# One decoder block on one core: in four groups of the feed-forward, VectorE instead of TensorE turns the other half of the hidden tiles

## The chip, the cores and the metric

The kernel runs on one NeuronCore of a Trainium2 chip, as one program and one launch. The metric is device time in microseconds (us), the median over runs of the same kernel. An engine is named by its role: TensorE (PE in the profile; its weight loads are PEld), VectorE (DVE), ScalarE (ACT), GpSimd (POOL), SyncE (SP), which issues nearly all DMAs.

## The reference

A decoder block on x of 512 tokens by 1,024 channels, float32: a token mixer of two branches (retention and forgetting attention), then the feed-forward that this change touches.

```python
        x = x + merged @ w_out[l]
        h2 = rmsnorm(x, g_ffn[l])
        ff = (jax.nn.silu(h2 @ w_gate[l]) * (h2 @ w_up[l])) @ w_down[l]
        x = x + ff
```

w_gate and w_up are 1,024 by 2,816, w_down is 2,816 by 1,024.

## The kernel before, in words

Every float32 operand of a large product is split into a high part (a cast to the matmul format, on ScalarE) and a low part (the rest, on VectorE), and a product is the sum of three matmuls: high by high, low by high, high by low.

**Gate and up.** The 2,816 hidden columns are taken in six groups, g = 0 to 4 of 512 columns and g = 5 of 256. A group's result is a 2 by 2 block product over halves of the tokens and halves of the weights, done in seven block products instead of eight. Their operands on the token side (A11, A12, A21, A22 and the sums S1 to S4) stand ready in `xfh` and `xfl`; those on the weight side are the blocks B11, B12, B21, B22, loaded for each group by SyncE, and sums of them that VectorE makes in place (`sum_of`, L947). Each weight block has two halves, v = 0 and 1. `part` makes high and low of one half (ScalarE's cast L938, VectorE's subtraction L939, called "low" below) in a ring of three buffers (`ring_parts`), so the cast of a half waits until the matmuls on the half three before it are through.

`gu` is one block product: four k-tiles j by two token tiles tp by three terms, 24 matmuls with a 128x128 stationary tile and 512 moving columns. The first 12 use half v = 0, the last 12 half v = 1. In a group the products follow one another as A12 (into the banks `y_`, tile name sc), A11 (`x_`), S1 (`z_`), S2 (`x_`), S3 (`x_`), S4 (`z_`), A22 (`x_`); `x_`, `z_` have the tile name acc. S2 and S3 go on adding in the banks that the product before left, so `keep` (ScalarE, L1048) first copies those banks to `us`. TensorE's order is pinned as the code is written (`mm`, `turn`); VectorE's mostly by `queue`; SyncE issues DMAs in code order, and a DMA that must wait holds all behind it; the rest of ScalarE's order is the scheduler's.

**Turning the hidden tiles.** `hs[g]` holds four tiles of 128 tokens by 512 hidden columns (they lie in `us`). The product with w_down needs them with hidden columns on partitions, in `pf`. In groups 1 to 4 (for the tiles of group g - 1 = 0 to 3) the columns are handled in two ways. The first two of the four 128-column tiles go through TensorE: `put_h` issues eight 128x128 transposes (L75, into bank tp) between the products A12 and A11, and two ScalarE copies (L1023) bring them to `pf`. The last two go through VectorE: `turn_squares` turns 32x32 squares (L1030) of a token tile, tokens 0 and 1 ahead of S1's sums, tokens 2 and 3 between the low parts of S2, into the tile `squares`, and `put_squares` has SyncE place them with 16 DMAs of 32 KB (L1037). The tiles of groups 4 and 5 go through TensorE alone.

After the groups, `prepare` and `p_sums` split the tiles of `pf` for the product with w_down.

Of the kernel before, what the change touches and what calls it, by code (L numbers as in the profile page):

```python
# [17 lines left out]
P = 128  # L18
# [35 lines left out]
def block_kernel(ctx: ExitStack, tc, x, xT, c_early, c_tab, c_late, w_qf, w_tok, w_vg, w_a, w_y, w_o, w_gu, w_gl, w_dn, w_dh, out):  # L54
# [880 lines left out]
    def part(raw, pinned_=True):  # L935
        w2 = raw.shape[-1]
        h, l = (f[:, :w2] for f in ring_parts())
        nc.scalar.copy(out=h, in_=raw)  # L938
# [14 lines left out]
    def gu(os, parts, slot, new, w, by_bank=False, middle=None):  # L953
        steps = [(j, tp) for j in range(4) for tp in range(2)]
        for i, (j, tp) in enumerate(sorted(steps, key=lambda s: s[1]) if by_bank else steps):
# [9 lines left out]
    parts_of = {}  # L965

    def prepare(k):
# [14 lines left out]
        ph, pl = hl[:, 0, :], hl[:, 1, :]  # L982
        prepare.last = nc.scalar.copy(out=ph, in_=pf[:, k, :])
        if n > 0:
            after(prepare.last, cast)
        prepare.low = tt(out=pl, in0=pf[:, k, :], in1=f32(ph), op=ALU.subtract)
        parts_of[k] = (h, l, ph, pl)

    def p_sums(j):

        fx = wq.tile([P, 4, HT], F32, name="fx", tag="b1")
        a11, a21, a12, a22 = (pf[:, 2 * j + m2, s2 * HT:s2 * HT + HT] for m2 in range(2) for s2 in range(2))
# [5 lines left out]
        split_x(j, slice(A12, A22 + 1), pf[:, 2 * j + 1, :].rearrange("p (s t) -> p s t", s=2))  # L998
# [19 lines left out]
    def put_h(g, cs):  # L1018
        for c in cs:
# [3 lines left out]
            nc.scalar.copy(out=pf[:, 4 * g + c, :], in_=pb)  # L1023
# [3 lines left out]
    def turn_squares(g, ts):  # L1027

        for t in ts:
            queue(nc.vector.transpose(out=squares[g].rearrange("p b c t j -> p c b t j")[:, :, :, t, :], in_=hs[g][t][:, 2 * P:4 * P].rearrange("p (c b j) -> p c b j", c=2, b=4)))  # L1030

    def put_squares(g):

        for a in range(4):
            for b in range(4):
                to = pf[32 * b:32 * b + 32, 4 * g + 2:4 * g + 4, :].rearrange("p c (t a j) -> p (c t) a j", t=NT, a=4)
                nc.sync.dma_start(out=to[:, :, a, :], in_=squares[g][32 * a:32 * a + 32, b].rearrange("p c t j -> p (c t) j"))  # L1037
# [4 lines left out]
    for g, w in enumerate(GROUPS):  # L1042
# [3 lines left out]
        def keep(slot, os):  # L1046
            for tp in range(2):
                nc.scalar.copy(out=us[tp][:, slot, :], in_=os[tp][:, :w])  # L1048

        if g == 0:  # L1050
# [7 lines left out]
            pf = fp.tile([P, NF, S], F32, name="pf")  # L1058
        else:
            gu(y_, ahead[g], A12, True, w)  # L1060
            put_h(g - 1, (0, 1))
            second = [ahead[g, 1], part(raws[g][B11][1])]
            if g - 1 in SQUARES:
                squares[g - 1] = xp.tile([P, 4, 2, NT, 32], F32, name="squares", tag="s4")
                turn_squares(g - 1, (0, 1))
# [30 lines left out]
        parts = sums_in_parts(g, B12, B22)  # L1096
        if g == 0:
# [4 lines left out]
        gu(x_, parts, S3, False, w)  # L1102
        keep(2, x_)
        parts = [part(raws[g][B22][v]) for v in range(2)]
        if g + 1 < len(GROUPS):
            load_group(g + 1, (B22,))
        gu(z_, parts, S4, False, w)
        parts = sums_in_parts(g, B11, B21)
        if g + 1 < len(GROUPS):
            load_group(g + 1, (B11,))  # L1110
        for tp in range(2):
# [3 lines left out]
        gu(x_, parts, A22, False, w, by_bank=True)  # L1115
# [267 lines left out]
```

## Time and profile before

| what | us |
|---|---|
| median of 3 runs | 702.68 (702.62 to 703.54) |
| profiled execution | 702.11 |
| its span, first to last instruction | 700.3 |
| TensorE busy in the span | 693.4 (99%) |
| VectorE, ScalarE, GpSimd busy | 526.7, 372.0, 72.7 |

The span is what the profiler's records cover; the other 1.8 us lie around it. A matmul's record is longer than its turn on the engine, since matmuls overlap: the pace is read from one start to the next. "Busy" of TensorE says therefore only that something was in flight.

### The profile page before, as it was taken

What the parts mean: (1) busy time and instruction counts of PE and PEld (TensorE: products, weight loads), DVE (VectorE), ACT (ScalarE), POOL (GpSimd) and SP (SyncE); (2) the same over time, 40 slices, a digit from 0 to 9 for tenths busy, and PEclk for the clock granted to TensorE, in tenths of its full rate; (3) what the DMA queues carried; (4) which work ended last, traced back from release to release, by engine and by line L of the source; (5) the groups of instructions that cost most, each with busy time, mean ns of one, the idle gap of its engine ahead of it and who ended that gap; (6) DMA issues with size and microseconds to landing.
All of it is one profiled execution on the core that took longest, in us unless ns stands there. A gap on an engine that the chain in (4) does not pass through costs nothing.

```text
span 700.3 us, 9534 instructions
## 1 busy us (share of the span) xinstructions
PE 693.4 (99%) x3567; PEld 579.6 (83%) x3567; DVE 526.7 (75%) x861; ACT 372.0 (53%) x562; POOL 72.7 (10%) x90
## 2 busy tenths in 40 slices
PE   9999999999999999999999999999999999999997
PEld 6878988888878777888887888888888898888997
DVE  6898487754788776648979897878888878457694
ACT  6767353232567666325566665565656576344341
POOL 0004940201122120000130000000000000000000
PEclk9999999999999999999999999999999999999999
DMA  8900412222433311238411506153341533321321
GB/s 278 420 28 31 122 61 91 83 82 93 135 108 90 105 62 61 90 117 299 185 61 34 208 11 217 43 150 121 73 168 23 157 121 105 119 77 61 100 81 62
DMA packets 41551, 79.40 MB, mean 113 GB/s; under 512 B 20248, under 2 KB 20888, under 8 KB 40992
## 3 DMA queue, kind: packets, MB, share of 16 engines
q1 hardware_dynamic: 41360, 78.77, 33.3%
q8 instruction: 28, 0.46, 0.3%
q14 instruction: 19, 0.16, 0.1%
q10 hardware_dynamic: 144, 0.02, 0.0%
HBM read 73.52 MB, written 2.11 MB: 108 GB/s over the span
## 4 chain that ended last, share of the span: by engine, by line
PE 94%; DVE 2%; ACT 1%; DMA 1%; issue 1%; POOL 0%; SPq 0%; POOLq 0%; DVEq 0%; ACTq 0%
PE acc L72 70%; PE sc L72 16%; PE tp L72 5%; PE tp L75 3%; DMA raw<-in_w_tok_dram 1%; POOL cb L680 0%; DMA cb<-cd 0%; DVE tq L667 0%; DVE pr L688 0%; DVE sg L737 0%; DVE wl L155 0%; ACT ps L938 0%; ACT tk L659 0%; DVE pr L692 0%; DVE blk L407 0%
## 5 line engine op out<-in xcount | busy, mean ns | idle before, releaser
L72 PE MATMUL acc<-ps,xfh 128*128 128x512 f32 (+1 forms) x576 | 169.1, 374 | 0.1
L72 PEld LDWEIGHTS acc<-ps,xfh 128*128 128x128 f32 x576 | 105.2, 188 | 21.8 <-ACT us L1048 2.4
L939 DVE TENSOR_TENSOR ps<-b,ps 128x1024 fp32r<-128x1024 f32 (+1 forms) x84 | 94.8, 1136 | 30.4 <-ACT ps L938 29.2
L938 ACT CAST ps<-b 128x1024 fp32r<-128x1024 f32 (+1 forms) x84 | 82.5, 982 | 51.6 <-PE acc L72 36.2
L72 PE MATMUL acc<-ps,xfl 128*128 128x512 f32 (+1 forms) x288 | 107.1, 372 | 0.0
L154 ACT CAST wh<-raw 128x1024 fp32r<-128x1024 f32 (+1 forms) x44 | 46.1, 1049 | 85.1 <-PE acc L72 80.7
L155 DVE TENSOR_TENSOR wl<-raw,wh 128x1024 fp32r<-128x1024 f32 (+1 forms) x44 | 57.8, 1315 | 17.6 <-ACT wh L154 17.5
L72 PEld LDWEIGHTS acc<-ps,xfl 128*128 128x128 f32 x288 | 54.3, 188 | 8.9
L72 PE MATMUL acc<-xh,wh 128*128 128x512 f32 x128 | 53.2, 416 | 0.0
L947 DVE TENSOR_TENSOR b<-b,b 128x1024 f32<-128x1024 f32 (+1 forms) x48 | 52.1, 1126 | 0.0
L72 PE MATMUL acc<-wh,xh 128*128 128x512 f32 (+2 forms) x144 | 50.4, 350 | 0.0
L72 PE MATMUL acc<-xh,wl 128*128 128x512 f32 x128 | 50.2, 392 | 0.0
L72 PE MATMUL acc<-xl,wh 128*128 128x512 f32 x128 | 50.0, 390 | 0.0
L72 PE MATMUL acc<-wh,xl 128*128 128x512 f32 (+2 forms) x144 | 49.4, 343 | 0.0
L72 PE MATMUL acc<-wl,xh 128*128 128x512 f32 (+2 forms) x144 | 49.3, 342 | 0.0
L72 PE MATMUL acc<-hl,ps 128*128 128x512 f32 x168 | 40.4, 389 | 0.0
L72 PEld LDWEIGHTS acc<-hl,ps 128*128 128x128 f32 x168 | 31.5, 188 | 6.6
L1048 ACT COPY us<-acc 128x512 f32<-128x512 f32 (+1 forms) x48 | 26.5, 552 | 18.6 <-PE acc L72 17.0
L977 DVE TENSOR_TENSOR ps<-raw,ps 128x1024 fp32r<-128x1024 f32 x14 | 17.1, 1223 | 21.6 <-ACT ps L974 21.6
L72 PEld LDWEIGHTS acc<-wh,xh 128*128 128x128 f32 x144 | 27.2, 189 | 3.5 <-ACT wh L154 0.2
L72 PEld LDWEIGHTS acc<-wh,xl 128*128 128x128 f32 x144 | 27.2, 189 | 3.2
L72 PEld LDWEIGHTS acc<-wl,xh 128*128 128x128 f32 x144 | 27.2, 189 | 2.9
(298 smaller groups left out, 1491.5 us busy)
## 6 DMA issues: line engine op xcount, KB each, us to landing
b<-in_w_gu_dram SPq DMA_DIRECT2D x40, 512.0 KB, 4.4
raw<-in_w_a_dram SPq DMA_DIRECT2D x16, 512.0 KB, 3.6
raw<-in_w_dn_dram SPq DMA_DIRECT2D x14, 512.0 KB, 4.3
blk<-in_w_vg_dram SPq DMA_DIRECT2D x8, 512.0 KB, 10.4
raw<-in_w_tok_dram SPq DMA_DIRECT2D x8, 512.0 KB, 3.6
raw<-in_w_y_dram SPq DMA_DIRECT2D x8, 512.0 KB, 3.5
raw<-in_w_o_dram SPq DMA_DIRECT2D x8, 512.0 KB, 3.7
raw<-in_w_dh_dram SPq DMA_DIRECT2D x4, 1024.0 KB, 4.8
```

The costliest lines, as they stand in the source:

```text
L72: in_order(nc.tensor.matmul(o, **kw))
L75: in_order(nc.tensor.transpose(out=o, in_=src, identity=ident))
L154: split_raw.last = (nc.scalar.copy(out=h[:, :width], in_=raw[:, :width]), tt(out=l[:, :width], in0=raw[:, :width], in1=f32(h)[:, :width], ...
L155: tt(out=l[:, :width], in0=raw[:, :width], in1=f32(h)[:, :width], op=ALU.subtract))
L938: nc.scalar.copy(out=h, in_=raw)
L939: low = tt(out=l, in0=raw, in1=f32(h), op=ALU.subtract)
L947: queue(tt(out=raws[g][b][v], in0=raws[g][b][v], in1=raws[g][c][v], op=ALU.add))
L977: tt(out=l, in0=raw, in1=f32(h), op=ALU.subtract)
L1048: nc.scalar.copy(out=us[tp][:, slot, :], in_=os[tp][:, :w])
```

## The change

- In groups 1 to 4, `put_h` is not called. `turn_squares` turns whole token tiles (512 columns instead of 256), and the tile `squares` holds half of the tokens at a time, in the same 4 KB of a partition (tag s4) twice a group. Token tiles 0 and 1 are turned where they were; token tiles 2 and 3 are turned in the third product's time, one ahead of each half of B22's parts.
- `put_squares` issues 16 DMAs of 32 KB for each half, 32 a group instead of 16: the first 16 behind the loads of B21, the second 16 in pieces of 5, 7 and 4 around the loads of B22 and B11 of the next group.
- The copies of A11's, S2's and S3's results (`keep` with slots 0, 1, 2) are placed by order behind the second cast of the parts made next (`part.cast`); in group 0 only that of S3.
- `gu` takes S2 and S3 with `by=2`: pairs of k-tiles, (j 0, 1 of tp 0), (j 0, 1 of tp 1), (j 2, 3 of tp 0), (j 2, 3 of tp 1), instead of alternating tp at each j. `by=4` is the earlier `by_bank`.
- `pf` is laid out with the token half ahead of the tile number.

```diff
-    def gu(os, parts, slot, new, w, by_bank=False, middle=None):
+    def gu(os, parts, slot, new, w, by=1, middle=None):
+
         steps = [(j, tp) for j in range(4) for tp in range(2)]
-        for i, (j, tp) in enumerate(sorted(steps, key=lambda s: s[1]) if by_bank else steps):
+        for i, (j, tp) in enumerate(sorted(steps, key=lambda s: (s[0] // by, s[1], s[0]))):
...
+    def turn_squares(g, t):
+
+        to = squares[g, t // 2].rearrange("p b c t j -> p c b t j")[:, :, :, t % 2, :]
+        queue(nc.vector.transpose(out=to, in_=hs[g][t].rearrange("p (c b j) -> p c b j", c=4, b=4)))
+
+    def place_of_squares(g, half):
+        squares[g, half] = xp.tile([P, 4, 4, 2, 32], F32, name="squares", tag="s4")
+
+    def put_squares(g, half, which=range(16)):
+
+        for i in which:
+            a, b = i // 4, i % 4
+            to = pf[32 * b:32 * b + 32, half, 4 * g:4 * g + 4, :].rearrange("p c (t a j) -> p (c t) a j", t=2, a=4)
+            nc.sync.dma_start(out=to[:, :, a, :], in_=squares[g, half][32 * a:32 * a + 32, b].rearrange("p c t j -> p (c t) j"))
...
-            put_h(g - 1, (0, 1))
+            if g - 1 not in SQUARES:
+                put_h(g - 1, (0, 1))
             second = [ahead[g, 1], part(raws[g][B11][1])]
             if g - 1 in SQUARES:
-                squares[g - 1] = xp.tile([P, 4, 2, NT, 32], F32, name="squares", tag="s4")
-                turn_squares(g - 1, (0, 1))
+                place_of_squares(g - 1, 0)
+                for t in range(2):
+                    turn_squares(g - 1, t)
                 gu(x_, second, A11, True, w)
...
         if g - 1 in SQUARES:
-            sums = [sum_of(g, B11, B22, v) for v in range(2)]
-            parts = [part(sums[0])]
-            turn_squares(g - 1, (2, 3))
-            parts.append(part(sums[1]))
-            put_squares(g - 1)
-        else:
-            parts = sums_in_parts(g, B11, B22)
-        gu(x_, parts, S2, False, w)
-        keep(1, x_)
+            put_squares(g - 1, 0)
+        parts = sums_in_parts(g, B11, B22)
+        gu(x_, parts, S2, False, w, by=2)
+        if g == 0:
+            keep(1, x_)
...
         parts = sums_in_parts(g, B12, B22)
+        if g:
+            keep(1, x_, part.cast)
...
-        gu(x_, parts, S3, False, w)
-        keep(2, x_)
-        parts = [part(raws[g][B22][v]) for v in range(2)]
+        gu(x_, parts, S3, False, w, by=2)
+        if g - 1 in SQUARES:
+            place_of_squares(g - 1, 1)
+        parts = []
+        for v in range(2):
+            if g - 1 in SQUARES:
+                turn_squares(g - 1, 2 + v)
+            parts.append(part(raws[g][B22][v]))
+        keep(2, x_, part.cast)
+        if g - 1 in SQUARES:
+            put_squares(g - 1, 1, range(5))
         if g + 1 < len(GROUPS):
             load_group(g + 1, (B22,))
+        if g - 1 in SQUARES:
+            put_squares(g - 1, 1, range(5, 12))
```

On TensorE, at the end of product A12 of group 1 (banks sc) and the start of A11 (banks acc); us_3534 and us_3535 are the two tiles of `us`, ctab holds the identity:

```order
 L72 MATMUL sc<-ps,xfl 128x512
 L72 MATMUL sc<-ps,xfh 128x512
-L75 MATMUL tp<-ctab,us_3534 128x128
-L75 MATMUL tp<-ctab,us_3535 128x128
...
 L72 MATMUL acc<-ps,xfh 128x512
 L72 MATMUL acc<-ps,xfl 128x512
```

The eight transposes are gone and A11 follows A12 directly; the same in groups 2 to 4.

On VectorE in group 2, from the turn of token tiles 0 and 1 to the low parts of S4, before. b_4066, b_3996 and b_4031 are the blocks B11, B12 and B22; L947 are sums in place (x2: both halves), L939 low parts:

```order
L1030 STREAM_TRANSPOSE squares<-us_3534 128x2x4x32
L1030 STREAM_TRANSPOSE squares<-us_3535 128x2x4x32
L947 TENSOR_TENSOR b_4066<-b_4066,b_3996 128x1024 x2
L939 TENSOR_TENSOR ps<-b_4066,ps 128x1024 x2
L947 TENSOR_TENSOR b_4066<-b_4066,b_4031 128x1024 x2
L939 TENSOR_TENSOR ps<-b_4066,ps 128x1024
L1030 STREAM_TRANSPOSE squares<-us_3534 128x2x4x32
L1030 STREAM_TRANSPOSE squares<-us_3535 128x2x4x32
L939 TENSOR_TENSOR ps<-b_4066,ps 128x1024
...
L939 TENSOR_TENSOR ps<-b_4031,ps 128x1024 x2
```

And of the changed kernel (B11, B12 and B22 are b_4067, b_3982 and b_4025 there):

```order
L1034 STREAM_TRANSPOSE squares<-us_3534 128x4x4x32
L1034 STREAM_TRANSPOSE squares<-us_3535 128x4x4x32
L947 TENSOR_TENSOR b_4067<-b_4067,b_3982 128x1024 x2
L939 TENSOR_TENSOR ps<-b_4067,ps 128x1024 x2
L947 TENSOR_TENSOR b_4067<-b_4067,b_4025 128x1024 x2
L939 TENSOR_TENSOR ps<-b_4067,ps 128x1024 x2
...
L1034 STREAM_TRANSPOSE squares<-us_3534 128x4x4x32
L939 TENSOR_TENSOR ps<-b_4025,ps 128x1024
L1034 STREAM_TRANSPOSE squares<-us_3535 128x4x4x32
L939 TENSOR_TENSOR ps<-b_4025,ps 128x1024
```

The first pair of turns is twice as wide in its old place; the second pair left S2's low parts and stands, twice as wide, one ahead of each low part of S4.

On SyncE from group 1 to the loads that follow its turns, before (b_3996, b_4031, b_4066, b_4194: the next blocks B12, B22, B11 and the B21 after that):

```order
L1037 DMA pf<-squares 32x8x32 x16
L927 DMA b_3996<-in_w_gu_dram 128x1024 x2
L927 DMA b_4031<-in_w_gu_dram 128x1024 x2
L927 DMA b_4066<-in_w_gu_dram 128x1024 x2
L927 DMA b_4194<-in_w_gu_dram 128x1024 x2
```

And of the changed kernel (the same four blocks are b_3982, b_4025, b_4067, b_4187):

```order
L1044 DMA pf<-squares 32x8x32 x16
L927 DMA b_3982<-in_w_gu_dram 128x1024 x2
L1044 DMA pf<-squares 32x8x32 x5
L927 DMA b_4025<-in_w_gu_dram 128x1024 x2
L1044 DMA pf<-squares 32x8x32 x7
L927 DMA b_4067<-in_w_gu_dram 128x1024 x2
L1044 DMA pf<-squares 32x8x32 x4
L927 DMA b_4187<-in_w_gu_dram 128x1024 x2
```

Sixteen more DMAs stand in SyncE's queue, twelve of them ahead of the load of the next B11. On ScalarE the eight copies L1023 of groups 1 to 4 are gone; at a group's end the second gate activation (L1125) now stands ahead of the cast of the next B11's first half, where it stood behind it in groups 2 to 4; and the cast of `prepare`'s first hidden tile (on VectorE its low part) moved from group 4 to group 5.

## Rows read from the trace of the kernel before

**Rows 1.** From the page: busy time of the engines; the clock that TensorE was granted, in tenths of full speed, in 40 equal slices of the span; and the chain of work that ended last, by engine.

```profile
PE 693.4 (99%) x3567; PEld 579.6 (83%) x3567; DVE 526.7 (75%) x861; ACT 372.0 (53%) x562; POOL 72.7 (10%) x90
...
PEclk9999999999999999999999999999999999999999
...
PE 94%; DVE 2%; ACT 1%; DMA 1%; issue 1%; POOL 0%; SPq 0%; POOLq 0%; DVEq 0%; ACTq 0%
```

**Rows 2.** Timeline of TensorE (start, duration, engine, line, operation, out<-in, shape, count): the first matmul of A12 in group 1 and in group 5; and, of A22 of group 1, which goes bank by bank, a matmul near the start and the last, 22 matmuls later.

```profile
399.08 0.39 PE L72 MATMUL sc<-ps,xfh 128*128 128x512 f32 x1
...
556.38 0.28 PE L72 MATMUL sc<-ps,xfh 128*128 128x256 f32 x1
...
433.18 0.39 PE L72 MATMUL acc<-ps,xfl 128*128 128x512 f32 x1
...
438.17 0.39 PE L72 MATMUL acc<-ps,xfh 128*128 128x512 f32 x1
```

**Rows 3.** Timeline of TensorE in group 2, from the last matmul of A12 over the transposes into A11; and the row of the transposes from the view of line L75 (duration ns min/median/max, first and last start).

```profile
443.61 0.40 PE L72 MATMUL sc<-ps,xfh 128*128 128x512 f32 x1
443.84 1.04 PE L75 MATMUL tp<-ctab,us 128*128 128x128 f32 x8
444.64 0.47 PE L72 MATMUL acc<-ps,xfh 128*128 128x512 f32 x1
444.95 0.39 PE L72 MATMUL acc<-ps,xfl 128*128 128x512 f32 x1
...
L75 PE MATMUL tp<-ctab,us x56: 270/272/273, 404.5 to 583.7; 128*128 128x128 f32 x56
```

**Rows 4.** The end of S2 and the start of S3 in group 2: TensorE's matmuls (the row at 460.86 holds the last of S2 and the first of S3), then the weight load that waited; and two rows of the view of waits in 360 to 600 us (who waited for whom: us in total, times, longest).

```profile
460.63 0.39 PE L72 MATMUL acc<-ps,xfl 128*128 128x512 f32 x1
460.86 0.89 PE L72 MATMUL acc<-ps,xfh 128*128 128x512 f32 x2
461.58 0.40 PE L72 MATMUL acc<-ps,xfl 128*128 128x512 f32 x1
...
461.24 0.19 PEld L72 LDWEIGHTS acc<-ps,xfh 128*128 128x128 f32 x1 [0.42 <-ACT us L1048]
...
PEld acc L72 <- ACT us L1048: 2.4, 6, 0.4
...
PEld acc L72 <- DVE ps L939: 0.3, 1, 0.3
```

**Rows 5.** Timeline of ScalarE in group 2: the cast of the second half for S1, the two casts for S3, the copies of `keep` at S2's end; and at the end of the group the cast of the next B11's first half and the gate activation. In brackets: idle time before, and what ended it.

```profile
447.73 1.05 ACT L938 CAST ps<-b 128x1024 fp32r<-128x1024 f32 x1 [1.17 <-PE acc L72]
...
457.90 2.21 ACT L938 CAST ps<-b 128x1024 fp32r<-128x1024 f32 x2 [0.23 <-DVE b L947]
460.60 1.26 ACT L1048 COPY us<-acc 128x512 f32<-128x512 f32 x2 [0.49 <-PE acc L72]
...
477.99 1.06 ACT L938 CAST ps<-b 128x1024 fp32r<-128x1024 f32 x1 [0.31 <-PE acc L72]
478.94 0.68 ACT L1125 ACTIVATE us<-acc,rstd 128x512 f32<-128x512 f32 x1
```

**Rows 6.** Timeline of VectorE in group 2: the low part of B11's second half, the turns, the sums and low parts for S1; later the low parts of S3 and of S4.

```profile
442.40 1.22 DVE L939 TENSOR_TENSOR ps<-b,ps 128x1024 fp32r<-128x1024 f32 x1 [0.35 <-ACT ps L938]
443.55 0.76 DVE L1030 STREAM_TRANSPOSE squares<-us 128x256 f32<-128x256 f32 x2
444.23 2.31 DVE L947 TENSOR_TENSOR b<-b,b 128x1024 f32<-128x1024 f32 x2
446.59 1.23 DVE L939 TENSOR_TENSOR ps<-b,ps 128x1024 fp32r<-128x1024 f32 x1
448.81 1.22 DVE L939 TENSOR_TENSOR ps<-b,ps 128x1024 fp32r<-128x1024 f32 x1 [0.99 <-ACT ps L938]
...
458.99 2.38 DVE L939 TENSOR_TENSOR ps<-b,ps 128x1024 fp32r<-128x1024 f32 x2
462.85 1.23 DVE L939 TENSOR_TENSOR ps<-b,ps 128x1024 fp32r<-128x1024 f32 x1 [1.48 <-ACT ps L938]
465.43 1.23 DVE L939 TENSOR_TENSOR ps<-b,ps 128x1024 fp32r<-128x1024 f32 x1 [1.36 <-ACT ps L938]
```

**Rows 7.** From the views of lines L1030 and L1112: VectorE's turn of 256 columns, and a float32 difference of two tiles that occurs with 256 and with 512 columns (duration ns min/median/max).

```profile
L1030 DVE STREAM_TRANSPOSE squares<-us x16: 401/420/439, 404.5 to 532.5; 128x256 f32<-128x256 f32 x16
...
L1112 DVE TENSOR_TENSOR us<-us x12: 419/684/686, 394.9 to 576.1; 128x512 f32<-128x512 f32 x10, 128x256 f32<-128x256 f32 x2
```

**Rows 8.** SyncE's queue: timeline of group 2 (the 16 placing DMAs; the two loads of the next B11 and the two of the B21 after it); the placing DMAs' issue times from the view of line L1037, and their time from issue to landing; the latter for the weight loads L927 in 400 to 475 us.

```profile
454.28 10.74 SPq L1037 DMA_DIRECT2D pf<-squares  x16
...
472.16 1.75 SPq L927 DMA_DIRECT2D b<-in_w_gu_dram  x4
...
L1037 SPq DMA_DIRECT2D pf<-squares x64: 586/609/1690, 415.0 to 543.8; - x64
...
DMA to landing us min/median/max: 1.9/1.9/3.6
...
DMA to landing us min/median/max: 3.4/5.2/6.2
```

**Rows 9.** Timeline of ScalarE in group 5 (256 columns): the two casts for S3 and the copies of `keep` at S2's end.

```profile
568.23 1.25 ACT L938 CAST ps<-b 128x512 fp32r<-128x512 f32 x2
569.45 0.73 ACT L1048 COPY us<-acc 128x256 f32<-128x256 f32 x2
```

More of the change, by code (lines that the diff above doesn't have):

```diff
@@ L937, in part @@
         h, l = (f[:, :w2] for f in ring_parts())
-        nc.scalar.copy(out=h, in_=raw)
+        part.cast = nc.scalar.copy(out=h, in_=raw)
         low = tt(out=l, in0=raw, in1=f32(h), op=ALU.subtract)
@@ L965, in block_kernel, with h_tile @@
     parts_of = {}
+    def h_tile(k):
+        return pf[:, :, k, :]
     def prepare(k):
@@ L981, in prepare @@
               else prepare.hl[:, 2 * (n % 4) - 4:2 * (n % 4) - 2, :])
-        ph, pl = hl[:, 0, :], hl[:, 1, :]
-        prepare.last = nc.scalar.copy(out=ph, in_=pf[:, k, :])
+        ph, pl = (hl[:, i, :].rearrange("p (s t) -> p s t", s=2) for i in range(2))
+        prepare.last = nc.scalar.copy(out=ph, in_=h_tile(k))
         if n > 0:
             after(prepare.last, cast)
-        prepare.low = tt(out=pl, in0=pf[:, k, :], in1=f32(ph), op=ALU.subtract)
-        parts_of[k] = (h, l, ph, pl)
+        prepare.low = tt(out=pl, in0=h_tile(k), in1=f32(ph), op=ALU.subtract)
+        parts_of[k] = (h, l, hl[:, 0, :], hl[:, 1, :])
     def p_sums(j):
         fx = wq.tile([P, 4, HT], F32, name="fx", tag="b1")
-        a11, a21, a12, a22 = (pf[:, 2 * j + m2, s2 * HT:s2 * HT + HT] for m2 in range(2) for s2 in range(2))
+        a11, a21, a12, a22 = (pf[:, s2, 2 * j + m2, :] for m2 in range(2) for s2 in range(2))
         after(tt(out=fx[:, 0, :], in0=a21, in1=a22, op=ALU.subtract), prepare.low)
@@ L997, in p_sums @@
         after(split_x(j, A11, a11), prepare.last)
-        split_x(j, slice(A12, A22 + 1), pf[:, 2 * j + 1, :].rearrange("p (s t) -> p s t", s=2))
+        split_x(j, slice(A12, A22 + 1), h_tile(2 * j + 1))
         split_x(j, slice(S1, S3 + 1), fx[:, 0:3, :])
@@ L1022, in put_h @@
                 turn(pb[:, t * P:(t + 1) * P], hs[g][t][:, c * P:(c + 1) * P])
-            nc.scalar.copy(out=pf[:, 4 * g + c, :], in_=pb)
+            nc.scalar.copy(out=h_tile(4 * g + c), in_=pb.rearrange("p (s t) -> p s t", s=2))
     SQUARES = range(4)
[L1027 to L1037, printed above, removed]
+    def turn_squares(g, t):
[8 more added lines that the diff above has]
+            nc.sync.dma_start(out=to[:, :, a, :], in_=squares[g, half][32 * a:32 * a + 32, b].rearrange("p c t j -> p (c t) j"))
     squares = {}
@@ L1044, in block_kernel, with keep @@
         x_, z_, y_ = [bank("acc") for _ in range(2)], [bank("acc") for _ in range(2)], [bank("sc") for _ in range(2)]
-        def keep(slot, os):
+        def keep(slot, os, behind=None):
             for tp in range(2):
-                nc.scalar.copy(out=us[tp][:, slot, :], in_=os[tp][:, :w])
+                copy = nc.scalar.copy(out=us[tp][:, slot, :], in_=os[tp][:, :w])
+                if behind:
+                    after(copy, behind)
         if g == 0:
@@ L1068, in block_kernel @@
                 gu(x_, second, A11, True, w, middle=lambda: put_h(g - 1, (2, 3)))
-            keep(0, x_)
             parts = sums_in_parts(g, B11, B12)
+            keep(0, x_, part.cast)
         if g + 1 < len(GROUPS):
@@ L1110, in block_kernel @@
             load_group(g + 1, (B11,))
+        if g - 1 in SQUARES:
+            put_squares(g - 1, 1, range(12, 16))
         for tp in range(2):
@@ L1114, in block_kernel @@
             ahead[g + 1] = [part(raws[g + 1][B21][0])]
-        gu(x_, parts, A22, False, w, by_bank=True)
+        gu(x_, parts, A22, False, w, by=4)
         for tp in range(2):
@@ L1238, in block_kernel @@
             ws.append(factors(w_dh[g + 1]))
-        o = pf[:, HALF + 2 * g:HALF + 2 * g + 2, :].rearrange("p a (s t) -> p (a s) t", s=2)
+        o = pf[:, g % 2, HALF + 4 * (g // 2):HALF + 4 * (g // 2) + 4, :]
         rows = [out[m * P:(m + 1) * P, :] for m in (2 * g, 2 * g + 1)]
```

2 lines of the change are left out of this document (1 added, 1 removed).

## The prediction, written before the changed kernel was run

> **What bounds the kernel now.** I read the busy times first, the granted clock next, then the chain that ended last [rows 1]: TensorE is busy in 99% of the span, its clock is full in every slice, and the chain is TensorE for 94%. So a time is won only where TensorE issues something that need not be there, or stands still. The view to look at is therefore TensorE's timeline in the groups, from one matmul's start to the next. Where nothing disturbs it, 22 matmuls take 438.17 - 433.18 = 4.99 us, 0.2268 us each [rows 2]; a group of 512 columns has 7 x 24 = 168 of them, 38.1 us. The four groups 1 to 4, the ones that are changed, run from 399.08 to 556.38 [rows 2], 157.30 us, where 4 x 168 x 0.2268 = 152.42 would do. So 4.88 us, 1.22 a group, are lost there. Two disturbances hold them.
>
> - The transposes. The last matmul of A12 starts at 443.61, A11's first only at 444.64, and its second comes 0.31 after instead of 0.23 [rows 3]. That is 444.95 - 443.61 - 2 x 0.227 = 0.89 us.
> - The copies. S3 adds into the banks of S2, and its first weight load waits for `keep`'s copy (0.42 idle; six such waits, 2.4 us together) [rows 4]. Two of the steps are long: from 460.86 to 461.58 there are two steps and the engine should need 0.454; it loses 0.27.
>
> 0.89 + 0.27 = 1.16; the other 0.06 is a slightly slower pace in the ten or so matmuls behind each interruption, which goes with them.
>
> **Term 1, transposes removed: -3.7.** Four times 0.89, and about half of the 0.06: 4 x 0.92 = 3.7. It counts only if A11 can start at once behind A12. What it needs is there: the low part of B11's second half, the last of its inputs, starts at 442.40 and takes 1.22 [rows 6], so it ends at 443.62, ahead of A12's end. The profile's 272 ns a transpose [rows 3] is a latency; eight occupy 0.80 from the first to A11's first matmul. The Trainium skill, page "TensorE: Matmul & The Clock Gate", Part 4: PE-mode transpose, gives about 275 ns for a transpose inside a kernel. The trace's duration agrees with it, but by that price 32 of them would give 8.8 us and the kernel 692.3; the start-to-start row decides, and I leave that 2 chances in 100.
>
> **Term 2, the wait between S2 and S3: -1.5.** By pairs, bank tp 0 is complete after 18 of 24 matmuls instead of 21, 0.68 us earlier, so its copy could start 0.68 earlier than 460.60 [rows 5], at 459.92. But `keep` now stands behind both casts; they end at 457.90 + 2.21 = 460.11 [rows 5], and a following instruction starts up to 0.1 before its predecessor's end there. So the copy runs about 460.05 to 460.65 instead of 460.60 to 461.19. The weight load that waited at 461.24 would, one step of 0.227 behind its neighbours, be due at 460.86. It fits, by 0.2 us. The second copy follows at 461.28 as before and is wanted only six matmuls (1.36 us) into S3. The casts' own time hangs on TensorE's middle of S1 and on VectorE behind it, and moves with TensorE. So 0.27 + 0.03 goes in each of groups 0 to 4: 5 x 0.30 = 1.5. In group 5 it stays: there the copy at 569.45 follows the casts (568.23 + 1.25 = 569.48) without a gap [rows 9], so an earlier bank doesn't help. That TensorE goes as fast when it stays in a bank is shown by A22 [rows 2].
>
> **Term 3, group 0: -0.1.** Its one wait for a low part (0.3 of a weight load [rows 4], 0.1 between matmuls) stands behind a cast that came late, after a copy; in the new order the cast goes first.
>
> **Added on VectorE: 0.** Eight turns of 256 columns in each pair of halves become four a group of 512. The trace has no turn of 512; one of 256 takes 420 ns, and a difference of two tiles takes 419 with 256 columns and 684 with 512 [rows 7]. So I take 0.68 (0.65 from start to start); the bounds are 0.42 and twice that, 0.84. In the old place the pair costs 1.3 to 1.5 instead of 0.68 (443.55 to 444.23 [rows 6]). With TensorE's A11 starting at 443.84, S1 starts 24 x 0.2268 = 5.44 later, at 449.28, and its third matmul needs the first low part, so by 449.5 with the weight load. VectorE: turns from 443.55 to 444.85, two sums 2.36 to 447.2, low part 1.23 to 448.4 (448.8 with the wide bound). Spare: 0.7 to 1.1 us. A turn would have to take over 1.17 to be felt. The second pair stands where VectorE idled 1.48 and 1.36 us waiting for casts [rows 6], one turn in each gap. ScalarE only loses work (eight copies).
>
> **Added on SyncE: 0.** Sixteen placing DMAs took 10.74, 0.67 each, and land 1.9 after issue (3.6 at most) [rows 8]. All on the clock of group 2 before: the first half's go from 444.9 to 455.6 and have landed by 457.5; the second half's first turn, which reuses their tile, comes behind S3's low parts, at about 460.3. The second half's 5 start behind its last turn, at about 464.0 (the S4 parts of 462.85 and 465.43 [rows 6], 0.9 earlier, and a turn); with the loads of B22 and the 7 behind them (12 x 0.67 + 0.9), the next B11 is issued at 473.0 instead of 472.16, and its first half lands 3.5 later, at 476.5. TensorE's A22 then ends at 449.28 - 5.44 + 6 x 5.44 = 476.5 as well, and the cast of that half stands behind the activation of 0.68 [rows 5], so at 477.4. It is there 0.9 before, and the cast may be 1.4 later still before A11 or the sums of S1 feel it. The last four DMAs land by 478.6, the next turn comes at 481.6.
>
> **The sum.** 3.7 + 1.5 + 0.1 = 5.3 off the profiled execution's 702.11: 696.8. The median of the runs is 0.57 above that execution, so **697.4**. Its own range is 696.7 to 698.3.
>
> **The rivals.**
>
> 1. The copy still comes late: `keep` behind two casts. For it: the margin is 0.2 us and the casts wait on VectorE (0.23 before 457.90 [rows 5]). Against: that chain has lost a pair of turns between S2's low parts. Then only terms 1 and 3 stay, 3.8 off: 698.9.
> 2. Slower: SyncE's queue. Twelve more DMAs stand ahead of the next B11, which has 0.9 + 1.4 = 2.3 us of room. If a placing DMA held the queue not 0.67 but p us, B11 is late by 12 x (p - 0.67) - 2.3 a group, and A11 with it, four times; the 5.3 are gone at p = 0.97, and at p = 1.1 the time is 697.4 + 4 x 2.9 = 709. For it: single issues of 1.69, landings of 3.6, loads that take 6.2 when they share the queues [rows 8]. Against: the sixteen in a row at 0.67, and half of them already in the kernel without a wait of TensorE for them. The Trainium skill, page "DMA: Bandwidth & Descriptors", Rules for kernel authors, speaks against the change in the same sense: transfers under 64 KB pay mostly overhead and should be merged, and here 64 more of 32 KB are issued. The overhead is there (0.67 us and 1.9 to land, for what is a small part of a load's time), but no row so far shows an engine waiting for it.
> 3. VectorE becomes late in S1: at 1.5 us a turn, 0.65 a group, 2.6 of the gain: 700.0. For it: VectorE is busy three quarters of the span [rows 1], more in the groups. Against: 420 ns for 256 columns is what any float32 operation of that size takes [rows 7].
> 4. The waits only move: TensorE's 0.9 goes, and the next wait for a cast or low part in A11 or S1 takes it back. That is no change, about 702. Against: every input of A11 is ready before A12 ends, as above.
>
> **Chances.** The forecast 0.68; rival 1 0.13 (698.5 to 699.4); rival 2 0.07 (702 and above); rival 3 0.07 (699 to 701.5); rival 4 0.03; the deeper gain 0.02. The range 696.5 to 699.8 takes in the forecast, rival 1 and the nearer half of rival 3, and leaves out under 0.2. A measurement of this kernel tells 0.2%, 1.4 us, from no change: faster means under 701.3. Faster 0.88, same 0.05, slower 0.07.
>
> **What would show it.** Term 1: no L75 in groups 1 to 4 and a start-to-start of 0.23 from the last sc matmul to the first acc one. Term 2: five of the six waits of weight loads for L1048 gone, one (group 5) left. A group's period of 38.1 to 38.2 instead of 39.3. VectorE: turns of about 0.68; no wait of TensorE for L939 or L938 in S1. SyncE: the next B11 issued about 1 us later in its group, its cast not waiting for the DMA. Wrong it would be if ScalarE's cast of B11 waits for its load, if a turn waits for DMAs, or if the period stays over 38.6.

## The result, and the profile after

The changed kernel took 696.71 us (median of 5 runs, 696.29 to 697.00); its ratio to the kernel before, run beside it, is 0.9908 with a 95% interval of 0.9894 to 0.9921. That is 696.2 us on the scale of the 702.68 (695.2 to 697.1). (The ratio of the two medians alone is 0.9915, inside the interval.) It is faster, as forecast, and by more: 6.0 us by the medians and 6.5 by the ratio, where 5.3 were forecast. Measured again twice later, the same kernel gave 0.9923 (0.9911 to 0.9936) and 0.9927 (0.9914 to 0.9940), 697.3 and 697.6. The profiled execution took 696.29, its span is 694.0.

From the page after: busy times and the chain, to be laid beside [rows 1].

```profile
PE 688.2 (99%) x3535; PEld 577.0 (83%) x3535; DVE 531.2 (77%) x861; ACT 367.6 (53%) x554; POOL 73.0 (11%) x90
...
PE 94%; DVE 3%; DMA 1%; ACT 1%; issue 1%; POOL 1%; SPq 0%; DVEq 0%; POOLq 0%
```

TensorE has 32 instructions fewer and is as fully busy as before; VectorE went from 526.7 to 531.2, ScalarE from 372.0 to 367.6. The groups 1 to 4 by windows of one group each, from A12's first matmul to the next (us, then busy us of each engine, granted clock, DMA share, GB/s):

```profile
398.26:436.34 38.08, 38.08 (x170) 31.53 (x168) 34.67 (x37) 21.77 (x26) 0.00 (x0) 1.00 0.41 110
436.34:474.42 38.08, 38.08 (x170) 31.53 (x168) 34.74 (x37) 21.76 (x26) 0.00 (x0) 1.00 0.51 142
474.42:512.50 38.08, 38.08 (x170) 31.53 (x168) 34.74 (x37) 21.75 (x26) 0.00 (x0) 1.00 0.47 129
512.50:550.58 38.08, 38.08 (x170) 31.53 (x168) 34.47 (x37) 21.00 (x26) 0.00 (x0) 1.00 0.39 103
```

All four take 38.08 us, which is 168 matmuls of 0.2267: nothing interrupts TensorE in them any more. Before they took 157.30 together [rows 2], now 152.32. Both places in group 2, timeline of TensorE (start, duration):

```profile
441.55 0.39 PE L72 MATMUL sc<-ps,xfh 128*128 128x512 f32 x1
441.78 0.39 PE L72 MATMUL acc<-ps,xfh 128*128 128x512 f32 x1
442.00 0.39 PE L72 MATMUL acc<-ps,xfl 128*128 128x512 f32 x1
...
457.64 0.39 PE L72 MATMUL acc<-ps,xfl 128*128 128x512 f32 x1
457.87 0.61 PE L72 MATMUL acc<-ps,xfh 128*128 128x512 f32 x2
458.32 0.39 PE L72 MATMUL acc<-ps,xfl 128*128 128x512 f32 x1
```

From A12's last matmul to A11's first it is 0.23 (1.03 in [rows 3]), and over the border of S2 and S3 two steps take 0.45 (0.72 in [rows 4]). Of the waits of weight loads for `keep`'s copies one is left in 360 to 600 us, in group 5; there were six in the same stretch [rows 4]:

```profile
PEld acc L72 <- ACT us L1055: 0.2, 1, 0.2
```

The engines that took over. ScalarE at S3's casts and at the next B11's cast, VectorE's first pair of turns, both in group 2; the view of line L1034 (turns; duration ns min/median/max); SyncE's queue in group 2, and the view of line L1044 (issue of a placing DMA, ns):

```profile
454.91 2.21 ACT L938 CAST ps<-b 128x1024 fp32r<-128x1024 f32 x2 [0.23 <-DVE b L947]
457.03 0.58 ACT L1055 COPY us<-acc 128x512 f32<-128x512 f32 x1
...
474.62 0.69 ACT L1146 ACTIVATE us<-acc,rstd 128x512 f32<-128x512 f32 x1 [0.26 <-PE acc L72]
475.21 1.04 ACT L938 CAST ps<-b 128x1024 fp32r<-128x1024 f32 x1
```

```profile
441.49 1.30 DVE L1034 STREAM_TRANSPOSE squares<-us 128x512 f32<-128x512 f32 x2
...
L1034 DVE STREAM_TRANSPOSE squares<-us x16: 668/704/705, 403.4 to 537.2; 128x512 f32<-128x512 f32 x16
```

```profile
461.74 3.21 SPq L1044 DMA_DIRECT2D pf<-squares  x5
465.05 1.02 SPq L927 DMA_DIRECT2D b<-in_w_gu_dram  x2
466.11 4.51 SPq L1044 DMA_DIRECT2D pf<-squares  x7
470.72 1.02 SPq L927 DMA_DIRECT2D b<-in_w_gu_dram  x2
...
L1044 SPq DMA_DIRECT2D pf<-squares x128: 585/609/1283, 404.8 to 550.2; - x128
```

The copy of S2's first bank follows the casts without a gap, as forecast; the pair of turns takes 1.30; the cast of the next B11 stands right behind the activation here, with no wait for its load. For group 4 it does wait; the row of the view of waits in 395 to 600 us:

```profile
ACT ps L938 <- DMA b<-in_w_gu_dram: 0.5, 1, 0.5
```

SyncE's queue had stood 1.2 us in group 3, until a load of B22 was there that took 6.4 to land. So B11 was issued 1.4 us later in its group than in group 2, and its cast starts at 513.86, 1.36 behind the start of A12 instead of 0.78. Group 4 takes 38.08 even so: TensorE does not feel it. The other two profiles of this kernel show the same wait for group 4 (0.2 and 0.6).

### The profile page after: what moved, and what is told of

Read it like the earlier page. It is cut to its first block, busy times and chain, and to the rows that moved or that the text cites. A ratio compares the mean times of both kernels' runs of the same rounds, so it can differ in the third digit from the quotient of the medians.

```text
span 694.0 us, 9527 instructions
## 1 busy us (share of the span) xinstructions
PE 688.2 (99%) x3535; PEld 577.0 (83%) x3535; DVE 531.2 (77%) x861; ACT 367.6 (53%) x554; POOL 73.0 (11%) x90
## 3 DMA queue, kind: packets, MB, share of 16 engines
HBM read 73.52 MB, written 2.11 MB: 109 GB/s over the span
## 4 chain that ended last, share of the span: by engine, by line
PE 94%; DVE 3%; DMA 1%; ACT 1%; issue 1%; POOL 1%; SPq 0%; DVEq 0%; POOLq 0%
PE acc L72 71%; PE sc L72 16%; PE tp L72 4%; PE tp L75 2%; DMA xf<-in_xT_dram 1%; POOL cb L680 1%; DMA cb<-cd 0%; DVE tq L667 0%; DVE pr L688 0%; DVE sg L737 0%; DVE xl L198 0%; ACT xh L196 0%; DVE wl L155 0%; ACT tk L659 0%; DVE pr L692 0%
## 5 line engine op out<-in xcount | busy, mean ns | idle before, releaser
L72 PE MATMUL acc<-ps,xfh 128*128 128x512 f32 (+1 forms) x576 | 166.9, 372 | 0.0
L939 DVE TENSOR_TENSOR ps<-b,ps 128x1024 fp32r<-128x1024 f32 (+1 forms) x84 | 94.5, 1135 | 20.6 <-ACT ps L938 19.3
L947 DVE TENSOR_TENSOR b<-b,b 128x1024 f32<-128x1024 f32 (+1 forms) x48 | 52.1, 1125 | 0.5 <-DMA b<-in_w_gu_dram 0.5
L981 DVE TENSOR_TENSOR ps<-raw,ps 128x1024 fp32r<-128x1024 f32 x14 | 17.1, 1222 | 21.7 <-ACT ps L978 21.7
```

Source lines behind the costliest of these rows:

```text
L72: in_order(nc.tensor.matmul(o, **kw))
L947: queue(tt(out=raws[g][b][v], in0=raws[g][b][v], in1=raws[g][c][v], op=ALU.add))
```

## The experiments

The times first. "Ratio" is to the kernel before, run beside it. The other columns come from one profile each: the start of group 0's A12, the time from there to group 1's A12, groups 1 to 4, from group 5's A12 to the last matmul's start, and what the span has behind that.

| kernel | median | ratio (95%) | ahead of group 0 | group 0 | groups 1-4 | to the last matmul | behind it |
|---|---|---|---|---|---|---|---|
| before | 702.68 | 1 | 364.68 | 34.40 | 157.30 | 140.10 | 3.81 |
| changed, first | 696.71 | 0.9908 (0.9894-0.9921) | 364.38 | 33.88 | 152.32 | 140.00 | 3.46 |
| changed, second | 697.24 | 0.9923 (0.9911-0.9936) | 365.45 | 33.87 | 152.32 | 140.08 | 3.45 |
| changed, third | 696.72 | 0.9927 (0.9914-0.9940) | 364.57 | 33.88 | 152.32 | 140.02 | 3.46 |
| transposes back | 700.59 | 0.9978 (0.9969-0.9987) | 364.78 | 33.88 | 155.96 | 140.03 | 3.46 |
| before, with pairs | 700.72 | 0.9971 (0.9962-0.9980) | 365.82 | 33.87 | 155.96 | 140.08 | 3.84 |
| no pairs | 698.75 | 0.9947 (0.9935-0.9960) | 365.35 | 34.16 | 153.56 | 140.15 | 3.45 |
| copies not ordered | 702.62 | 1.0003 (0.9994-1.0012) | 364.78 | 33.87 | 158.51 | 140.09 | 3.45 |
| first copies ordered | 696.16 | 0.9909 (0.9894-0.9924) | 365.18 | 33.88 | 152.32 | 140.09 | 3.53 |
| pair of turns twice | 698.65 | 0.9949 (0.9937-0.9962) | 365.07 | 33.87 | 154.43 | 140.04 | 3.45 |
| three times | 703.55 | 1.0017 (1.0008-1.0026) | 366.16 | 33.87 | 159.21 | 140.03 | 3.45 |
| places together | 705.84 | 1.0050 (1.0038-1.0063) | 364.64 | 33.87 | 159.75 | 141.35 | 3.45 |
| half of group 5 | 696.71 | 0.9920 (0.9908-0.9932) | 365.30 | 33.87 | 152.32 | 139.93 | 3.45 |

**1. The changed kernel again (second, third).** Is there more in it than the two interruptions?

> The changed kernel once more, nothing altered. Theory A (the gain is the two interruptions of TensorE, the transposes 4 x 0.90 = 3.6 and the wait between S2 and S3 5 x 0.33 = 1.65, with 0.2 of group 0's A22; what the times showed beyond these 5.5 is scatter between executions, ahead of the groups and behind the last matmul): ratio to before 0.992 (gain 5.5 us), and a second profile in which the groups 1 to 4 are again 152.3 us, while the stretch ahead of group 0 and the one behind the last matmul differ from the first profile by some tenths. Theory B (there is a third gain of about 0.9 us outside of these steps): ratio 0.991 or less again, and the same 0.3 ahead of the groups and 0.4 behind the last matmul as in the first profile.

> The changed kernel a third time, nothing altered, for the size of the gain: the first measurement gave a ratio of 0.9908 and the second 0.9923. If the gain is the 5.6 us that both traces show from group 0 to the last matmul: 0.9915 to 0.9925. If more than that is gained outside of the groups: 0.9908 or less.

From group 0's A12 to the last matmul the three profiles agree to 0.07 us: 326.20, 326.27 and 326.22, against 331.80 before. That is 5.5 to 5.6 less, theory A's number, though the third ratio, 0.9927, lies just above the 0.9915 to 0.9925 expected from it. Ahead of group 0, where the change touches nothing, the same kernel starts 364.38 in one execution and 365.45 in the next; over the profiles of the table it is 364.38 to 366.16. So the 0.3 us that the first profile has there is scatter. The 0.35 behind the last matmul is not: each kernel with the new placing has 3.45 to 3.53 there, the two with the old one 3.81 and 3.84. On that point theory B was right, with 0.35 of its 0.9.

**2. The transposes back (term 1).**

```diff
             if g - 1 not in SQUARES:
                 put_h(g - 1, (0, 1))
+            else:
+                for c in range(2):
+                    pb = bank("tp")
+                    for t in range(NT):
+                        turn(pb[:, t * P:(t + 1) * P], hs[g - 1][t][:, c * P:(c + 1) * P])
```

> The changed kernel, but with the eight transposes of TensorE put back between A12 and A11 in groups 1 to 4; they write a bank that nothing reads, so this is work added, and VectorE still turns all columns. It prices term 1 by itself. Theory A: 4 x 0.90 = 3.6 us slower than the changed kernel, that is 1.9 to 2.4 faster than before (ratio 0.9970), period of a group 38.98, no wait elsewhere. Theory B: about 0.9 us better than that, ratio 0.9957. If an interruption hides other waits (rival 4 of the prediction, in reverse), less than 3 us slower than the changed kernel.

Ratios: 0.0055 and 0.0051 above the later two measurements of the changed kernel, 3.6 to 3.9 us, and 0.0070 above the first, 4.9 us. The profile says it sharper, as the groups took 152.32 in all three profiles of the changed kernel: 155.96 - 152.32 = 3.64, 0.91 a group. Timeline of TensorE in group 2:

```profile
442.84 0.40 PE L72 MATMUL sc<-ps,xfh 128*128 128x512 f32 x1
443.08 1.04 PE L75 MATMUL tp<-ctab,us 128*128 128x128 f32 x8
443.87 0.47 PE L72 MATMUL acc<-ps,xfh 128*128 128x512 f32 x1
444.18 0.39 PE L72 MATMUL acc<-ps,xfl 128*128 128x512 f32 x1
```

From 442.84 to 444.18 it is 1.34, where two steps would take 0.45: 0.89, the very sum of [rows 3], and 0.02 in the steps behind. No other wait of TensorE came or went, so none was hidden behind the transposes.

**3. The pairs alone, and the change without them (term 2).** In one kernel `by=2` for S2 and S3 is all that is changed in the kernel before; in the other it is all that is taken out of the changed one.

```diff
-        gu(x_, parts, S2, False, w)
+        gu(x_, parts, S2, False, w, by=2)
```

> The kernel before with nothing but the order by pairs of k-tiles in S2 and S3; transposes, copies, placing and the layout of pf as before. It prices term 2 by itself. Theory A: ScalarE's copies stand behind the casts there already, so the weight loads of S3 no longer wait in groups 0 to 4: 1.5 to 1.8 us faster than before, ratio 0.9977. Theory B: the same. Rival 1 of the prediction (the copy still comes late): under 0.5 us faster, and the weight loads of S3 still wait for the copies.

> The changed kernel with S2 and S3 again k-tile by k-tile, alternating the two banks; all else as changed. Theory A: the wait between S2 and S3 is back, 5 x 0.33 = 1.65 slower than the changed kernel, gain over before 3.9, ratio 0.9945; period of a group 38.4. Theory B: 0.9 us better, ratio 0.9932. If the copies' place behind the casts is what removed the wait, and not the pairs: no slower than the changed kernel.

Waits of weight loads for the copies in 395 to 600 us, in the kernel before with pairs, then in the changed kernel without them:

```profile
PEld acc L72 <- ACT us L1048: 0.2, 1, 0.2
```

```profile
PEld acc L72 <- ACT us L1055: 2.4, 8, 0.4
```

The pairs are what takes the wait away, in either kernel. Groups 1 to 4 get shorter by 157.30 - 155.96 = 1.34 with them, 0.33 each; taken out of the changed kernel they cost 153.56 - 152.32 = 1.24, 0.31 each. Group 0 goes from 34.40 to 33.87 with pairs alone and to 34.16 in the changed kernel without them; so its one wait for a low part (0.2) is lifted by either edit, and the pairs are worth 0.3 beside it. The two edits add up, to 0.1: 3.64 + 1.34 is 4.98, what groups 1 to 4 won in all, and 3.64 + 1.24 is 4.88. And the kernel before with pairs takes the 155.96 of the changed kernel with its transposes back. TensorE's work is the same in both; the wider turns, the 16 more DMAs a group, the copies L1023 and the layout of `pf` are not. So what the change moved to or from the other engines cost nothing in these groups.

**4. The copies without an order.**

```diff
                 copy = nc.scalar.copy(out=us[tp][:, slot, :], in_=os[tp][:, :w])
-                if behind:
-                    after(copy, behind)
```

> The changed kernel without the rule that orders the keep copies behind the casts, so that in places a copy, which waits for its bank, stands between two casts of ScalarE. Theory A (the pairs alone took the wait between S2 and S3 away, the copies' place is worth only group 0's one wait, 0.2): 0 to 0.3 us slower than the changed kernel, ratio to before 0.9923 to 0.993. Rival (the place matters: a cast that stands behind a waiting copy makes a low part late): 1 us slower or more, with weight loads that wait for low parts or casts in S1 and S3.

The rival was right, and by far more than either side said: the whole gain is gone, 1.0003. Three of the groups take 40.12 to 40.16. ScalarE and TensorE in group 3, at the start of S1, and two rows of the view of waits:

```profile
487.25 0.59 ACT L1055 COPY us<-acc 128x512 f32<-128x512 f32 x1 [6.43 <-PE acc L72]
487.73 1.05 ACT L938 CAST ps<-b 128x1024 fp32r<-128x1024 f32 x1
```

```profile
487.50 0.39 PE L72 MATMUL acc<-ps,xfh 128*128 128x512 f32 x1
488.83 0.50 PE L72 MATMUL acc<-ps,xfh 128*128 128x512 f32 x1 [0.94 <-ACT ps L938]
...
490.09 0.73 PE L72 MATMUL acc<-ps,xfh 128*128 128x512 f32 x2 [0.53 <-DVE ps L939]
...
PEld acc L72 <- ACT ps L938: 4.1, 3, 1.4
PEld acc L72 <- DVE ps L939: 2.9, 3, 1.0
```

The copy of A11's first bank has come to stand ahead of the first cast for S1. It waits 6.43 us for its bank, nearly until A11 ends, and the cast, ready long before, waits behind it; S1 then waits 1.1 for the cast and 0.7 for its low part. It is not there in group 1, where the copy happens to stand behind the casts, and it was not there in the kernel before, which has no such rule either: there the order came out well unasked.

**5. Which copies the rule is for.** The rule stays for the copies of A11 and goes for those of S2 and S3.

```diff
-            keep(1, x_, part.cast)
+            keep(1, x_)
...
-        keep(2, x_, part.cast)
+        keep(2, x_)
```

> The changed kernel with the rule that puts copies behind casts kept for the copies of A11 alone (behind the casts for S1); those of S2 and S3 are free again, and between the two casts for S3 stands the first copy of S2 in groups 2 to 4. It asks which copies the rule is for. If the loss without any rule was all at the start of S1, where the trace without the rule shows it (2.0 us a group in groups 2 to 4): as the changed kernel, ratio to before 0.991 to 0.9925. If the place of the other copies matters too: 0.5 us or more slower than the changed kernel, with a wait of S3's weight loads for a cast or a low part.

152.32 again: this kernel (four runs) takes the changed one's time in every group, though S2's first copy now stands between the two casts for S3. The rule is needed in one place. The ratio of 0.9909 beside the 0.9927 of the changed kernel in the same comparison is the size of the scatter, as the profiles show no difference.

**6. More work on VectorE (rival 3).** The first half's pair of turns is done twice, and three times.

```diff
-                for t in range(2):
+                for t in (0, 1, 0, 1):
                     turn_squares(g - 1, t)
```

> The changed kernel with the first half's pair of turns done twice on VectorE, 1.30 us more work ahead of the sums and low parts of S1 in groups 1 to 4 (the second pair writes the same again). It measures the cover of rival 3 (VectorE late in S1). By the prediction's 0.7 to 1.1 us of spare time: 0.2 to 0.6 late a group, 0.8 to 2.4 slower than the changed kernel. By the trace after the change (first low part of S1 ends at 446.3, its matmul starts at 447.67): 1.35 spare, so 0 to 0.4 slower altogether, still no wait over 0.1 a group.

> As the run with the pair done twice, but three times: 2.60 us more on VectorE in the same place. By the trace after the change (1.35 spare): TensorE waits 1.25 a group for the first low part of S1, 5.0 us slower than the changed kernel, ratio to before 0.9995. By the prediction's 0.7 to 1.1: 6.0 to 7.6 slower. If VectorE has slack enough behind S1, the wait stays in S1 and is not repeated in S2.

Twice: 154.43 - 152.32 = 2.11, 0.53 a group, and TensorE does not wait in S1 at all. It waits where term 2 had freed it. ScalarE at the end of S2 in group 2, the weight load of S3, and the row of the waits:

```profile
456.96 2.21 ACT L938 CAST ps<-b 128x1024 fp32r<-128x1024 f32 x2 [0.44 <-DVE b L947]
459.07 1.07 ACT L1055 COPY us<-acc 128x512 f32<-128x512 f32 x2
...
459.70 0.19 PEld L72 LDWEIGHTS acc<-ps,xfh 128*128 128x128 f32 x1 [0.63 <-ACT us L1055]
...
PEld acc L72 <- ACT us L1055: 2.7, 5, 0.6
```

VectorE's sums for S3 come late, ScalarE's casts wait for them, and the copies, bound behind the casts, hold S3's weight load. Both rivals 1 and 3 named a half of this chain; neither put them together. The step at S3's first matmul is 0.60 instead of 0.23, so 0.37 of the 1.18 that VectorE really lost (2.48 for four turns, 1.30 for two) came through: 0.8 us was the spare time. Three times: 159.21 - 152.32 = 6.89, 1.72 a group, now with S1's waits as well, for the cast and for the low part (0.5 and 1.0 of a weight load), and with S3's again, which the expectation left out. In S1 TensorE loses 1.2 of the 2.37 added (3.67 for six turns), so the spare time of S1 itself was about 1.2, an estimate from these rows.

```profile
PEld acc L72 <- DVE ps L939: 3.9, 4, 1.0
...
PEld acc L72 <- ACT ps L938: 2.1, 4, 0.5
```

**7. SyncE's queue (rival 2).** First the second half's sixteen DMAs together, ahead of B22 and B11; then placing DMAs as two of half the size.

```diff
-            put_squares(g - 1, 1, range(5))
+            put_squares(g - 1, 1)
...
-            put_squares(g - 1, 1, range(5, 12))
...
-            put_squares(g - 1, 1, range(12, 16))
```

> The changed kernel with the second half's sixteen placing DMAs issued together, all ahead of the loads of B22 and B11, instead of 5, 7 and 4 around them. Four more stand ahead of the next B11: 4 x 0.64 = 2.6 us later on SyncE's queue. It measures the room of rival 2. By the prediction's room (2.3 us, of which the change itself used 1.0 to 1.4): 1.3 to 1.7 late a group, 5 to 7 us slower than the changed kernel. By the trace after the change (B11 lands 0.64 before its cast; the low part of that half could be up to 2.4 later before A11 feels it, the sums behind it on VectorE 1.35): 0 to 0.6 late a group, 0 to 2.4 slower.

Slower by more than either expectation, 0.0123 to 0.0142 above the changed kernel, 9 to 10 us. ScalarE and SyncE before group 2:

```profile
423.91 10.67 SPq L1044 DMA_DIRECT2D pf<-squares  x16
434.68 3.13 SPq L927 DMA_DIRECT2D b<-in_w_gu_dram  x6
```

```profile
436.79 0.69 ACT L1142 ACTIVATE us<-acc,rstd 128x512 f32<-128x512 f32 x1 [0.26 <-PE acc L72]
441.16 1.05 ACT L938 CAST ps<-b 128x1024 fp32r<-128x1024 f32 x1 [3.68 <-DMA b<-in_w_gu_dram]
```

Besides the four more issues, six loads now follow one another without a pause, and B11's first half lands 5.3 us after its issue (4.1 in the changed kernel). The cast, which stood at 437.12, starts at 441.16, 3.8 later beside the 0.25 by which this execution is late anyway. TensorE is 1.2 late once A11 is under way and 2.3 once S1 is. So the cast could have been about 1.5 later without harm to S1, which is the prediction's 1.4; what the expectations missed is the slower landing.

```diff
-            nc.sync.dma_start(out=to[:, :, a, :], in_=squares[g, half][32 * a:32 * a + 32, b].rearrange("p c t j -> p (c t) j"))
+            for c in range(2):
+                nc.sync.dma_start(out=to[:, 4 * c:4 * c + 4, a, :], in_=squares[g, half][32 * a:32 * a + 32, b].rearrange("p c t j -> p (c t) j")[:, 4 * c:4 * c + 4, :])
```

> The changed kernel with each placing DMA of the second half issued as two of 16 KB, 32 issues instead of 16, the bytes as before; 12 more issues stand ahead of the next B11. It asks what a placing DMA costs SyncE's queue. If an issue costs 0.64 us whatever its size: B11 is issued 7.7 us later; with the room that the run with the places together showed (about 1.5 to the sums of S1), some 5.5 to 6.5 late a group, 20 to 25 us slower than the changed kernel. If the issue costs by bytes or by pieces (so half of 0.64 each): the same time as the changed kernel, within 0.5 us.

The edit reaches further than the expectation: it splits the DMAs of both halves, 64 issues a group instead of 32, where 48 were meant; the trace has 256 of them (row below), the changed kernel 128. 750.31, ratio 1.0678 (1.0663 to 1.0692): 53 us slower than the changed kernel; groups 1 to 4 take 197.47. The chain that ended last by engine, the view of the DMAs' line, a row of the waits, and three windows at the start of A11 in group 2 (the column before the last two is the granted clock):

```profile
PE 59%; SPq 18%; DVE 9%; DMA 5%; issue 4%; ACT 4%; POOL 0%; DVEq 0%; ACTq 0%; POOLq 0%
...
L1045 SPq DMA_DIRECT2D pf<-squares x256: 585/599/1512, 406.2 to 607.6; - x128
...
DVE squares L1034 <- DMA pf<-squares: 29.7, 4, 8.1
```

```profile
448.00:453.00 5.00, 1.17 (x6) 0.62 (x4) 0.00 (x0) 0.69 (x1) 0.00 (x0) 0.92 0.70 221
453.00:459.00 6.00, 5.55 (x12) 4.00 (x13) 5.61 (x7) 1.56 (x3) 0.00 (x0) 0.50 0.59 189
459.00:469.00 10.00, 10.00 (x45) 8.26 (x45) 9.88 (x10) 7.39 (x10) 0.00 (x0) 1.00 0.17 29
```

A half costs the queue as much as a whole (0.60 against 0.61), so at these two sizes an issue has a price, not a byte. How late the group would be with the second half alone in pieces was not run, so the 20 to 25 us expected stand untested. From one issue to the next it is 0.64 to 0.67 here, so 64 of them need 41 to 43 us, an estimate, where a group of the changed kernel has 38.08: SyncE's queue alone cannot keep that time, and its issues are 18% of the chain. Besides, the late DMAs of the first half hold the tile that the second half's turn reuses (29.7 us in four waits), and TensorE, after it had stood for 4.25 us, went on at half clock for some five us. How the 53 us divide between these is not shown.

**8. A step further: half of group 5.** The transposes of group 4's tiles for the first half of the tokens go to VectorE too: `put_rest` makes four transposes of TensorE, for the second half of the tokens and two tiles of columns, where `put_h` made eight; `turn_last` is four turns of 256 columns on VectorE, and 16 placing DMAs follow behind the next stage's first two loads.

```diff
-                put_h(g - 1, (0, 1))
+                put_rest(g - 1, 0)
...
-                gu(x_, second, A11, True, w, middle=lambda: put_h(g - 1, (2, 3)))
+                turn_last(g - 1)
+                gu(x_, second, A11, True, w, middle=lambda: put_rest(g - 1, 2))
```

> The changed kernel carried on into group 5: of the 16 transposes that TensorE still does there for group 4's tiles, the eight of the first half of the tokens go to VectorE (four turns of 256 columns, 1.7 us, into free columns of the us tiles) and 16 placing DMAs that are issued behind the first loads of the next stage. If an interruption of TensorE is paid by the transpose here too (0.79 for eight in group 5): 0.8 us faster than the changed kernel, ratio to before 0.9910. If VectorE has no room there (about 1.5 us ahead of S1's low part in group 5, against 1.7 added): the same time, the gain turned into a wait for low parts or copies. Slower by 1 us or more only if the placing DMAs hold up the next stage's loads.

0.9920, the same as the changed kernel. TensorE's two interruptions shrink from 0.79 to 0.36 each, but VectorE has no room there. Of the waits in 395 to 600 us below, that for the copies was 0.2 before, that of TensorE itself for them and that for L939 are new; only the one for L981 was there already. So 0.75 of the 0.87 goes again, 0.4 in S1 and 0.35 in S3.

```profile
PEld acc L72 <- ACT us L1073: 0.6, 1, 0.6
PEld sc L72 <- DVE ps L981: 0.4, 1, 0.4
PE acc L72 <- ACT us L1073: 0.4, 1, 0.4
PEld acc L72 <- DVE ps L939: 0.3, 1, 0.3
```

## Why the prediction was right, and where it was not

- **Term 1, -3.7:** right; 3.64 by the transposes put back. The start-to-start row priced them. The Trainium skill, page "TensorE: Matmul & The Clock Gate", Part 4: PE-mode transpose, has about 275 ns for one, and the trace's duration of 272 agrees; taken as time that TensorE loses it would have been 8.8, and it was 0.1 each.
- **Term 2, -1.5:** right in mechanism, under by up to 0.13: 0.31 to 0.33 in each of groups 1 to 4 and 0.29 in group 0, 1.53 to 1.63 together, as the slower steps behind the wait were counted with 0.03 and are 0.04 to 0.06. The copy ran at 457.03, 0.16 ahead of what was worked out (460.05 less the 2.86 by which A11 came earlier is 457.19). Group 5 kept its wait, though 0.1 shorter.
- **Term 3, -0.1:** the wait is 0.24 with its slower steps; and it goes by either of two edits.
- **The sum, -5.3,** holds the step that failed: what comes behind the last matmul had no term, and so was put at nothing without a reason, and the waits of terms 2 and 3 were sized too small. Behind the last matmul the changed kernels end 0.35 sooner. The groups gave 5.60 (0.52 in group 0, 4.98 in groups 1 to 4, 0.10 from group 5's A12 on, which is 0.02 and 0.08 in the other two profiles): term 1 gave 0.06 less than its 3.7, the waits 1.96 where 1.6 were counted. Together 5.95, which is 696.7.
- **The range** had no room for that. The prediction shows no working for its low end, 696.5, 0.9 under the forecast, and did not look at the scatter between executions of one kernel: 1.8 us ahead of group 0 alone, and ratios of 0.9908 to 0.9927, 1.3 us, for one kernel. With 0.65 more gain than the sum and 0.5 of scatter the first measurement fell 0.3 under the low end. The other two lie inside; that they come nearer to 697.4 than the profiles' 5.95 does is scatter too, and no merit of the sum.
- **VectorE +0:** right; a turn of 0.70 (0.68 taken). But the limit stood in the wrong place: not the low parts of S1, which have about 1.2 us, but the copies of S2 behind ScalarE's casts give way first, at 0.8 us. The 0.7 to 1.1 forecast were for S1; that 0.8 lies among them is a coincidence of numbers.
- **SyncE +0:** right for TensorE, which never waited for B11, and wrong in the margin. B11 was to land 0.9 ahead of its cast; in group 2 it was 0.64 (470.72 and 3.85 to land, 475.21), and for group 4 the cast waited 0.5, which the prediction had named as a sign of being wrong. The room behind that cast covered it: 1.5 by the places put together, where 1.4 was forecast. What the step left out is how the loads land: with the places put together B11's first half is the third of six loads in a row, and it landed 1.2 us slower besides. The Trainium skill, page "DMA: Bandwidth & Descriptors", Rules for kernel authors, says that transfers under 64 KB pay mostly overhead; the traces agree so far as a placing DMA held the queue 0.60 us for 16 KB and 0.61 for 32. The change still pays, as SyncE had the time.
- **Not in the sum at all:** the rule that orders the copies. The prediction weighed it only as a risk (rival 1). It is what the gain stands on: without it 6.2 us are lost in groups 2 to 4, all of the gain. The forecast is not wrong by it, as the changed kernel has the rule; but only instructions that change were priced, and a rule that fixes an order which the kernel before had by itself looked free.

Of the rivals, none came with the change itself; rivals 1 and 3 came together, as one chain, once 1.2 us were added on VectorE. Rival 4 (the waits only move) is excluded by the four equal groups.

## To carry to other kernels

Price a removed interruption by starts, with and without it, never by the duration of what interrupts; such a price held to 0.02 us a group here. When work leaves an engine, look at what its absence does to the order of the rest: a copy that waits for a bank, come to stand ahead of a cast that waits for nothing, cost as much as the whole change won. And follow a spare time past the first user: it ended not where the work was added but two engines further, at the narrowest margin.

## What the runs showed that was not expected

- After a wait of 4.25 us TensorE was granted 0.50 (1.2 GHz) in the six us that follow, and full clock again after; in the other runs TensorE's waits in the groups were of up to 1.1 us, and the clock over the span was 0.999 to 1.0.
- A placing DMA of 16 KB and one of 32 KB hold SyncE's queue equally long, 0.60 and 0.61 us (medians).
- Behind the last matmul the changed kernels end 0.35 us sooner. SyncE's wait for the last output DMA ends 2.47 us behind that matmul's start in the kernel before and in the changed one, so it is not that the data land sooner. Nearly all of it lies between two semaphore instructions of SyncE that come next, for which no wait is recorded: 2.61 to 2.95 before, 2.59 to 2.63 after. What holds SyncE there was not tried and stays open.
